# Strided items earlier in the middle heads, and the merge statistics and weights in the idle PSUM bank of a strided item

## The chip, the cores and the metric

One core of one Trainium2 chip runs the whole program. The metric is the device time of one execution in microseconds (us).

## The reference

The program computes one layer of a hybrid decoder for a prompt of 2048 tokens and for a small sample group. The stage that matters here is the prompt's attention: 8 heads of 64 channels, and in each head three branches of dilated window attention, which are merged by their softmax denominators.

```python
BRANCHES = ((128, 1), (512, 4), (2048, 16))
...
    s = jnp.einsum('bnqrhc,bnkrhc->bnrhqk', qb, kc).astype(jnp.float32)
    s = s * (HEAD_DIM ** -0.5) + bias[None, None, None]
    s = jnp.where(valid[None, :, None, None], s, NEG_INF)
    lse = jax.nn.logsumexp(s, axis=-1)
    p = jnp.exp(s - lse[..., None])
    o = jnp.einsum('bnrhqk,bnkrhc->bnqrhc', p.astype(vc.dtype), vc)
...
def _merge_branches(outs, lses):
    w = jax.nn.softmax(jnp.stack(lses, axis=0), axis=0)
    return jnp.sum(w[..., None] * jnp.stack(outs, axis=0).astype(jnp.float32), axis=0)
```

## The kernel before

The attention stage stands between the projections and the output projection with its feed-forward block. A head has 20 **items**: 16 *band* items, one for each block of 128 queries, which do the branches of dilation 1 and 4 together over up to five key blocks; and 4 *strided* items, which do the branch of dilation 16, each for four of its sixteen residues. The list `OTHER` (L1124) gives the order of the items of heads 1 to 6, `FIRST` and `LAST` those of heads 0 and 7. One item is begun at each step of a plan, so a head is 20 steps; "place 7" is below the eighth item of a head.

Every piece of work is filed with `at(step, phase, function)`, and the plan issues it sorted by step, then by phase (`early, exp, low, scores, turn, mid, values, out, misc, store`). Nothing else sets the order: each engine runs its instructions as they were issued, and waits in place for what is not ready.

An item begun at step x goes through these stages:

- **band**: scores on PE at x (L881); bias and minimum on DVE at x + 1 (L887); exponential on ACT at x + 2 (L892); transposes on PE at x + 3 (L900), in one group of up to four, and for every odd block from 4 on a second group of two; copies of the high parts on ACT (L903), and the low parts `pl` on DVE at x + 4 (L922). Every four band items their products with the values follow, in three parts on three steps (L936), then a copy to `ob` on ACT (L945).
- **strided**: queries put in order on POOL at x - 3 (L865, into one buffer `qo`); scores on PE at x (L954); bias and minimum on DVE at x + 1 (L959, L961) and the subtraction on POOL (L962); exponential on ACT at x + 3 (L965); sum on DVE (L969) and four transposes on PE (L974) at x + 4, with the high part `eh` on ACT (L977); the low part `el` on DVE at x + 5, phase `mid` (L922); the values on PE at x + 6 or the next step that no band values take (L985, L986); a copy to `o` on ACT one step later (L993).

PSUM: scores are written to `ps_s`, two buffers of two banks each in turn. A band item uses up to 640 columns of the pair; a strided item uses bank 0 alone, and its bank 1 is idle. All transposes go in turn to three single banks, named `ps_t0`, `ps_t1` and `ps_o2` (`ps_a`). The values have one bank, `ps_o3`.

When a head is done, its **statistics** (`Stats`: a product on POOL, two small matmuls on PE at L1012, a copy on DVE) and its **weights** (`Weights`: a minimum on DVE at L1030, small operations on POOL, ACT and DVE, a transpose on PE at L1051, a copy and a store to DRAM `f_d` on ACT) are made during the next head. They too take a bank of the three. The weights are then loaded again for all partitions (`merge_load`, SP's queue, L1067), and POOL multiplies and adds the two outputs in four chunks of three operations (`merge`, L1078, L1080, L1082); the result is stored to `cat_d` (L1087).

Of the kernel before, what the change touches and what calls it, by code (L numbers as in the profile page):

```python
# [21 lines left out]
NT = T // P  # L22
# [21 lines left out]
class Plan:  # L44
# [21 lines left out]
def hymba_step(ctx: ExitStack, tc: tile.TileContext, A: dict, O: dict):  # L66
    nc = tc.nc
    sync, act, dve, pool, pe = nc.sync, nc.scalar, nc.vector, nc.gpsimd, nc.tensor
# [7 lines left out]
    turn = [0, 0, 0, 0]  # L76
# [3 lines left out]
    def ps_s():  # L80
        return psum_s.tile([P, 2, 512], F32, name="ps_s", tag="s", bufs=2)
# [22 lines left out]
    def ps_a():  # L104

        turn[2] = (turn[2] + 1) % 3
        return bank(turn[2])
# [53 lines left out]
    at = plan.at  # L161
# [490 lines left out]
    B0 = 240  # L652
# [49 lines left out]
    for half in range(2):  # L702
        for ki, kind in enumerate(ORDER[half]):
            for gi, tiles in enumerate(GROUPS):
# [13 lines left out]
                for j, tj in enumerate(tiles):  # L718
                    t = half * 8 + tj
                    e, ph = e0 + 2 * j, "out"  # L720
                    if last:
                        e, ph = e0, "early"
                    elif third:

                        e, ph = (e0 + 2 * j + 2, "out") if j < 2 else (e0, "early")
# [41 lines left out]
    for i, (b, t, u) in enumerate(key_units):  # L767
        s0 = key_steps[i]
# [11 lines left out]
    for bg in range(2):  # L780
        s0 = V0 - 8 + bg * 33
# [164 lines left out]

    def strided_scores(it):
        d, st, r4 = it["d"], it["st"], it["n"]
        it["s"] = s = ps_s()[:, 0, :]
        for a in range(4):  # L950
            k = by_residue(d["k"])[:, r4 * 4 + a]
            out = s[:, a * P:(a + 1) * P].rearrange("p (n m) -> p n m", m=RUN)
            for z in range(2):
                pe.matmul(out, it["q"][:, z, a], k, start=(z == 0), stop=(z == 1))  # L954
# [45 lines left out]
    class Stats:  # L1000
# [5 lines left out]
            self.eng.tensor_tensor(self.m, self.st[:, 4:6].unsqueeze(3).broadcast_to([P, 2, NT, RUN]),  # L1006
                                   sel_m.unsqueeze(1).unsqueeze(1).broadcast_to([P, 2, NT, RUN]), op=OP.mult)

        def b(self):
            self.p = pt = ps_a()  # L1010
            for z in range(2):
                pe.matmul(pt[:, z * NT:(z + 1) * NT], self.m[:, z].rearrange("p r m -> p (r m)"), sel_n, start=True, stop=True)  # L1012

# [107 lines left out]


    FIRST = list(range(10)) + ["s", 10, 11, "s", 12, 13, "s", 14, 15, "s"]
    OTHER = [0, 1, "s", 2, 3, 4, 5, "s", 6, 7, 8, 9, "s", 10, 11, 12, 13, "s", 14, 15]  # L1124

    LAST = [0, "s", 1, "s", 2, "s", 3, "s", 4, 5, 6, 7] + list(range(8, NT))
    items, taken = [], set()
# [25 lines left out]
    for h in range(1, H):  # L1153
# [3 lines left out]
        for y in (6, 7, 8, 9, 11, 13) if h == 1 else (1, 2, 3, 4, 10, 12):  # L1157
            at(s0 + y, "misc", load, h)
        at(s0 + 16, "misc", order_bias, h)
    def stats_of(h, eng, steps):  # L1160
        d = {}
        at(*steps[0], lambda: d.update(s=Stats(h, sts[h], eng)))
        for (y, ph), fn in zip(steps, "abc"):
            at(y, ph, lambda fn=fn: getattr(d["s"], fn)())
        return d

    def weights_of(d, steps, n0=0, n1=NT):
        w = {}
        at(*steps[0], lambda: w.update(w=Weights(d["s"], n0, n1)))
        for (y, ph), fn in zip(steps, "weights_a weights_b weights_c weights_d weights_e turn store".split()):  # L1170
            at(y, ph, lambda fn=fn: getattr(w["w"], fn)())
        return w

    def steps_of(s0, *steps):
        return [(s0 + y, ph) for y, ph in steps]

    last_half = {}
    for h in range(H):

        s0 = B0 + (h + 1) * NI  # L1180
        end = h == H - 1
        ahead = h == H - 2
        if end:

            x = s0 - NI
            d = stats_of(h, dve, steps_of(x, (11, "misc"), (13, "early"), (14, "early")))
            weights_of(d, steps_of(x, (14, "misc"), (15, "early"), *[(15, "misc")] * 3, (16, "early"), (16, "exp")), 0, NT // 2)
            for ch in range(2):
                at(x + 17, "mid", merge_load, h, ch)
                for part in range(3):  # L1190
                    at(x + 19 + part, "store", merge, h, ch, pool, part)
            last_half = weights_of(d, steps_of(s0, (3, "early"), (4, "early"), *[(4, "misc")] * 3), NT // 2, NT)
            continue
        if ahead:
            d = stats_of(h, pool, steps_of(s0, (2, "misc"), (4, "early"), (5, "early")))
            weights_of(d, steps_of(s0, (5, "misc"), (6, "early"), (6, "misc"), (7, "early"), (7, "misc"), (8, "early"), (8, "mid")))
            chunks = ((10, 13), (10, 16))
        else:
            d = stats_of(h, pool, steps_of(s0, (3, "misc"), (5, "early"), (6, "early")))
            weights_of(d, steps_of(s0, (6, "misc"), (7, "early"), (7, "misc"), (8, "early"), (8, "misc"), (10, "early"), (10, "mid")))  # L1200
            chunks = ((13, 16), (13, 19), (19, 22), (22, 25))

        for ch, (a, b) in enumerate(chunks):
            at(s0 + a, "mid", merge_load, h, ch)
            for part in range(3):
                at(s0 + b + part, "store", merge, h, ch, pool, part)
        if ahead:
            at(s0 + 19, "store", merge_store, h, 0, 2)
        else:
            at(s0 + 28, "store", merge_store, h, 0, 4)  # L1210
    last_s = [0]
    for i, it in enumerate(items):
        x, h, n = B0 + i, it["h"], it["n"]
# [605 lines left out]
    h = H - 1  # L1819
# [333 lines left out]
```

## Time and profile before

| what | value |
|---|---|
| median of 3 runs | 2627.35 us (2621.5 to 2628.19) |
| profiled execution: its own time | 2623.9 us |
| profiled execution: span from first to last instruction | 2621.9 us |
| mean granted TensorE clock | 0.977 |
| PE, DVE, ACT, POOL busy, of the span | 95%, 54%, 47%, 53% |

The span is 2.0 us shorter than the time of the same execution; this rest lies around it. The attention stage is from about 600 to 920 us of the span, and one middle head takes about 39 us, with PE, DVE and ACT all above three quarters busy. In a row of the timeline the columns are start, duration, engine, line, operation, output and inputs, count; the bracket gives the engine's idle time before it and what ended that.

### The profile page before, as it was taken

What the parts mean: (1) busy time and instruction counts of PE and PEld (TensorE: products, weight loads), DVE (VectorE), ACT (ScalarE), POOL (GpSimd) and SP (SyncE); (2) the same over time, 40 slices, a digit from 0 to 9 for tenths busy, and PEclk for the clock granted to TensorE, in tenths of its full rate; (3) what the DMA queues carried; (4) which work ended last, traced back from release to release, by engine and by line L of the source; (5) the groups of instructions that cost most, each with busy time, mean ns of one, the idle gap of its engine ahead of it and who ended that gap; (6) DMA issues with size and microseconds to landing.
All of it is one profiled execution on the core that took longest, in us unless ns stands there. A gap on an engine that the chain in (4) does not pass through costs nothing. (4 is left out here: it accounts for less than half of the span.)

```text
span 2621.9 us, 38941 instructions
## 1 busy us (share of the span) xinstructions
PE 2480.9 (95%) x13583; PEld 2188.5 (83%) x13583; DVE 1414.6 (54%) x2770; ACT 1221.5 (47%) x2570; POOL 1382.9 (53%) x1080
## 2 busy tenths in 40 slices
PE   8999899999999869999999999999999999999996
PEld 6777687678888758898999988999999987999995
DVE  4258675346888846434444366444444466444445
ACT  6414344446877626545454545432323336434332
POOL 2035754123667646676776743554544534666662
PEclk9999899999999989999999999999999999999998
DMA  8764844588787565455464564554453643555553
GB/s 251 217 212 155 277 141 128 180 261 245 202 234 225 143 176 171 141 182 176 141 204 142 181 185 157 169 186 171 159 203 132 221 149 123 194 204 201 197 194 109
DMA packets 313874, 481.05 MB, mean 183 GB/s; under 512 B 25907, under 2 KB 178916, under 8 KB 307792
## 3 DMA queue, kind: packets, MB, share of 16 engines
q1 hardware_dynamic: 308188, 469.53, 56.4%
q10 hardware_dynamic: 5492, 9.05, 1.2%
q8 instruction: 108, 1.77, 0.3%
q14 instruction: 86, 0.70, 0.1%
HBM read 382.76 MB, written 165.84 MB: 209 GB/s over the span
## 5 line engine op out<-in xcount | busy, mean ns | idle before, releaser
L1585 POOL TENSOR_TENSOR op<-fr,op 128x512 fp32r<-128x512 f32 x385 | 488.4, 1300 | 299.9 <-ACT op L1581 275.3
L1642 PE MATMUL ps_m<-xh,op 128*128 128x384 f32 (+4 forms) x1932 | 615.5, 319 | 3.7 <-DVE zn L1663 3.7
L1644 PE MATMUL ps_m<-xh,op 128*128 128x384 f32 (+4 forms) x1932 | 615.1, 318 | 1.6 <-POOL op L1585 1.6
L1643 PE MATMUL ps_m<-xl,op 128*128 128x384 f32 (+4 forms) x1932 | 614.2, 318 | 0.0
L1715 PE MATMUL ps_o<-dw,hw 128*128 128x512 f32 x2040 | 487.1, 393 | 18.0 <-DVE acc L1717 16.7
L1715 PEld LDWEIGHTS ps_o<-dw,hw 128*128 128x128 f32 x2040 | 381.1, 189 | 102.1 <-DVE acc L1717 23.8
L1642 PEld LDWEIGHTS ps_m<-xh,op 128*128 128x128 f32 x1932 | 368.6, 191 | 8.3 <-issue 2.7
L1643 PEld LDWEIGHTS ps_m<-xl,op 128*128 128x128 f32 x1932 | 368.4, 191 | 3.6
L1644 PEld LDWEIGHTS ps_m<-xh,op 128*128 128x128 f32 x1932 | 368.2, 191 | 2.0 <-POOL op L1585 1.9
L1717 DVE TENSOR_TENSOR acc<-acc,ps_o 128x512 f32<-128x512 f32 (+1 forms) x362 | 247.1, 687 | 215.8 <-PE ps_o L1715 215.8
L1682 ACT ACTIVATE ps_t<-zn 128x384 f32<-128x384 f32 (+1 forms) x126 | 58.3, 463 | 470.4 <-DVE zn L1665 367.8
L1581 ACT ACTIVATE op<-fr 128x512 fp32r<-128x512 f32 x396 | 235.3, 623 | 22.5 <-DMA fr<-ab_d 15.1
L138 POOL TENSOR_TENSOR dw<-fd,dw 128x1024 fp32r<-128x1024 f32 x66 | 158.8, 2406 | 124.3 <-ACT dw L135 119.6
L318 PE MATMUL ps_s<-wh,xh 128*128 128x512 f32 x480 | 198.4, 413 | 6.3 <-ACT xh L135 6.1
L319 PE MATMUL ps_s<-wl,xh 128*128 128x512 f32 x480 | 192.3, 401 | 0.0
L320 PE MATMUL ps_s<-wh,xl 128*128 128x512 f32 x480 | 191.8, 400 | 0.0
L1585 POOL TENSOR_TENSOR op<-pair,op 128x512 fp32r<-128x512 f32 x63 | 81.4, 1300 | 120.4 <-ACT op L1581 120.4
L1692 ACT ACTIVATE hw<-ps_t 128x384 fp32r<-128x384 f32 (+1 forms) x126 | 56.0, 453 | 175.4 <-DVE ps_t L1688 174.4
L318 PEld LDWEIGHTS ps_s<-wh,xh 128*128 128x128 f32 x480 | 93.0, 194 | 36.2 <-issue 8.4
L320 PEld LDWEIGHTS ps_s<-wh,xl 128*128 128x128 f32 x480 | 92.9, 193 | 20.7 <-DVE xl L138 0.2
L319 PEld LDWEIGHTS ps_s<-wl,xh 128*128 128x128 f32 x480 | 93.5, 195 | 18.0 <-DVE wl L226 0.5
L611 POOL TENSOR_TENSOR vl<-kv,vh 100x512 fp32r<-100x512 f32 (+1 forms) x32 | 46.0, 1439 | 110.1 <-ACT vh L605 37.9
(473 smaller groups left out, 4794.2 us busy)
## 6 DMA issues: line engine op xcount, KB each, us to landing
fr<-ab_d SPq DMA_DIRECT2D x308, 256.0 KB
fd<-in_w_down_dram SPq DMA_DIRECT2D x66, 512.0 KB
out_ks_dram<-in_cache_k_dram SPq DMA_DIRECT2D x56, 512.0 KB
out_vs_dram<-in_cache_v_dram SPq DMA_DIRECT2D x56, 512.0 KB
ab_d<-fr SPq DMA_DIRECT2D x88, 256.0 KB
raw<-in_w_in_dram SPq DMA_DIRECT2D x72, 256.0 KB
qk_d<-pair SPq DMA_DIRECT2D x64, 256.0 KB
ab_d<-pair SPq DMA_DIRECT2D x63, 256.0 KB
```

Source lines behind the costliest of these rows:

```text
L138: (eng_lo or pool).tensor_sub(lo, src, hi.bitcast(F32))
L318: pe.matmul(o[j], xh[:, k, :], wh, start=(k == 0), stop=False)
L319: pe.matmul(o[j], xh[:, k, :], wl, start=False, stop=False)
L320: pe.matmul(o[j], xl[:, k, :], wh, start=False, stop=(k == KD - 1))
L1581: act.activation(ops[f, j][0], ab[f][j], AF.Copy)
L1585: (pool if f or j in POOL_LOW else dve).tensor_sub(lo_, ab[f][j], hi.bitcast(F32))
L1642: pe.matmul(out, wh[:, ks], xh[:, :, k], start=(k == 0), stop=False)
L1643: pe.matmul(out, wh[:, ks], xl[:, :, k], start=False, stop=False)
L1644: pe.matmul(out, wl[:, ks], xh[:, :, k], start=False, stop=(k == 3))
L1682: act.activation(g, c, AF.Silu)
L1715: pe.matmul(ps[0:nr], l_, r_[:, cs], start=(z == 0 and y == 0), stop=(z == FC - 1 and y == len(pairs) - 1))
L1717: dve.tensor_add(B.acc[i][0:nr, cs], B.acc[i][0:nr, cs], ps[0:nr])
```

## The change

It does three things.

1. `OTHER` is written in another order: the strided items of heads 1 to 6 stand at places 1, 6, 11 and 15 instead of 2, 7, 12 and 17.
2. The statistics' matmuls and the weights' transpose of heads 0 to 6 write bank 1 of the `ps_s` pair of a strided item of the running head, right behind that item's scores, instead of a bank of the three.
3. Statistics, weights, merges and their store move in the plan: for heads 1 to 5 the statistics begin at place 19 of their own head instead of place 3 of the next, the weights are stored at place 7 instead of 10, and the merges run three steps sooner; for head 0 the merges begin one step later.

```diff
     def strided_scores(it):
         d, st, r4 = it["d"], it["st"], it["n"]
-        it["s"] = s = ps_s()[:, 0, :]
+        it["pair"] = ps_s()
+        it["s"] = s = it["pair"][:, 0, :]
...
-        def b(self):
-            self.p = pt = ps_a()
+        def b(self, place=None):
+            self.p = pt = (place or ps_a)()
...
-    OTHER = [0, 1, "s", 2, 3, 4, 5, "s", 6, 7, 8, 9, "s", 10, 11, 12, 13, "s", 14, 15]
+    OTHER = [0, "s", 1, 2, 3, 4, "s", 5, 6, 7, 8, "s", 9, 10, 11, "s", 12, 13, 14, 15]
...
+    def strided_bank(y):
+
+        return lambda: items[y - B0]["pair"][:, 1, :]
+
-    def stats_of(h, eng, steps):
+    def stats_of(h, eng, steps, spare=False):
         d = {}
         at(*steps[0], lambda: d.update(s=Stats(h, sts[h], eng)))
         for (y, ph), fn in zip(steps, "abc"):
-            at(y, ph, lambda fn=fn: getattr(d["s"], fn)())
+            args = (strided_bank(y),) if spare and fn == "b" else ()
+            at(y, ph, lambda fn=fn, args=args: getattr(d["s"], fn)(*args))
         return d
...
-        if ahead:
-            d = stats_of(h, pool, steps_of(s0, (2, "misc"), (4, "early"), (5, "early")))
-            weights_of(d, steps_of(s0, (5, "misc"), (6, "early"), (6, "misc"), (7, "early"), (7, "misc"), (8, "early"), (8, "mid")))
-            chunks = ((10, 13), (10, 16))
+        if h == 0:
+            d = stats_of(h, pool, steps_of(s0, (3, "misc"), (6, "turn"), (7, "early")), True)
+            weights_of(d, steps_of(s0, (7, "misc"), (8, "early"), (8, "misc"), (9, "early"), (9, "misc"), (11, "turn"), (12, "early")), spare=True)
+            chunks = ((14, 17), (14, 20), (20, 22), (22, 25))
         else:
-            d = stats_of(h, pool, steps_of(s0, (3, "misc"), (5, "early"), (6, "early")))
-            weights_of(d, steps_of(s0, (6, "misc"), (7, "early"), (7, "misc"), (8, "early"), (8, "misc"), (10, "early"), (10, "mid")))
-            chunks = ((13, 16), (13, 19), (19, 22), (22, 25))
-
+            d = stats_of(h, pool, steps_of(s0, (-1, "misc"), (1, "turn"), (2, "early")), True)
+            weights_of(d, steps_of(s0, (2, "misc"), (3, "early"), (3, "misc"), (4, "early"), (4, "misc"),
+                                   (7 if ahead else 6, "turn"), (8 if ahead else 7, "early")), spare=True)
+            chunks = ((10, 13), (10, 16)) if ahead else ((10, 13), (10, 16), (16, 19), (19, 22))
...
-            at(s0 + 28, "store", merge_store, h, 0, 4)
+            at(s0 + (28 if h == 0 else 25), "store", merge_store, h, 0, 4)
```

In the rows that follow, the numbers behind a name tell buffers apart; a line number is that of the kernel the row is from, and in the changed kernel the lines behind L948 stand one higher.

**The statistics' matmuls on PE, early in a middle head.** Before, they follow the first part of the band values, and the scores of the next band item follow them:

```order
L936 MATMUL ps_o3_7079<-pl_6915,ve_6222 128x512
L1012 MATMUL ps_t1_7090<-sel_n_5422,sm_7065 128x16 x2
L881 MATMUL ps_s_7098<-k_6493,qh_6463 128x384
L881 MATMUL ps_s_7098<-k_6493,qh_6463 128x256
L881 MATMUL ps_s_7098<-k_6493,ql_6520 128x384
L881 MATMUL ps_s_7098<-k_6493,ql_6520 128x256
```

In the changed kernel:

```order
L936 MATMUL ps_o3_6956<-pl_6792,ve_6231 128x256
L955 MATMUL ps_s_6994<-k_6506,qo_6925 128x128 x8
L1013 MATMUL ps_s_6994<-sel_n_5422,sm_6961 128x16 x2
L900 MATMUL ps_t1_7005<-ident_76,e_6930 128x128 x4
```

They have moved four steps ahead, behind the scores of the strided item at place 1, and write the same `ps_s` pair.

**A strided item's transposes on PE, and who takes their bank next: place 7 before, place 6 now.** Before, the transposes write `ps_t0`, and the next to write `ps_t0` are the last two of these rows:

```order
L974 MATMUL ps_t0_7264<-ident_76,e3_7171 128x128 x4
L900 MATMUL ps_t1_7272<-ident_76,e_7204 128x128 x4
L936 MATMUL ps_o3_7222<-ph_7049,v_6765 128x256
L936 MATMUL ps_o3_7222<-pl_7050,v_6765 128x256
L936 MATMUL ps_o3_7222<-ph_7049,v_6765 128x128
L936 MATMUL ps_o3_7222<-pl_7050,v_6765 128x128
L954 MATMUL ps_s_7288<-k_6493,qo_7225 128x128 x8
L900 MATMUL ps_o2_7297<-ident_76,e_7232 128x128 x4
L900 MATMUL ps_t0_7303<-ident_76,e_7204 128x128
L900 MATMUL ps_t0_7303<-ident_76,e_7232 128x128
```

In the changed kernel the bank is `ps_o2`:

```order
L975 MATMUL ps_o2_6686<-ident_76,e3_6615 128x128 x4
L900 MATMUL ps_t0_6694<-ident_76,e_6643 128x128 x4
L900 MATMUL ps_t1_6700<-ident_76,e_6584 128x128
L900 MATMUL ps_t1_6700<-ident_76,e_6643 128x128
L936 MATMUL ps_o3_6674<-ph_6522,ve_6231 128x384
L936 MATMUL ps_o3_6674<-pl_6523,ve_6231 128x384
L955 MATMUL ps_s_6724<-k_5951,qo_6659 128x128 x8
L900 MATMUL ps_o2_6733<-ident_76,e_6666 128x128 x4
```

The odd band item, with its second group of two transposes, now falls into the strided item's own step, so its bank comes round one group sooner. On DVE the rows that lead to `el`, the operation that frees this bank, were

```order
L969 TENSOR_REDUCE st_6462<-e3_7171 128x4
L887 ISA e_7285,st_6462<-ps_s_7259,bp_6873 128x640
L887 ISA st_6462 128x1
L922 TENSOR_TENSOR pl_7182<-ps_t1_7272,ph_7181 128x4x128
L922 TENSOR_TENSOR el_7270<-ps_t0_7264,eh_7269 128x512
L959 TENSOR_TENSOR e3_7311<-ps_s_7288,b_6541 128x512
```

and are now, for the item at place 11 (the same rows stand at place 6, with L887 in the place of L960 and L962):

```order
L970 TENSOR_REDUCE st_5917<-e3_6747 128x4
L960 TENSOR_TENSOR e3_6855<-ps_s_6820,b_6000 128x512
L962 TENSOR_REDUCE st_5917<-e3_6855 128x4
L922 TENSOR_TENSOR pl_6792<-ps_t1_6837,ph_6791 128x4x128
L922 TENSOR_TENSOR pl_6792<-ps_o2_6843,ph_6791 128x256
L922 TENSOR_TENSOR el_6835<-ps_t0_6829,eh_6834 128x512
```

A second low part has come in ahead of `el` at places 6 and 11, and at place 11 also the next strided item's bias and minimum, which stood behind it.

**The last strided item's exponential on ACT: place 17 before, place 15 now.** Before, two transposed copies stand between the previous strided item's output copy (L993) and the exponential (L965):

```order
L993 ACTIVATE o3_7202<-ps_o3_7465 128x4x16x8
L903 ACTIVATE ph_7457<-ps_t0_7484 128x4x128
L903 ACTIVATE ph_7457<-ps_t1_7490 128x256
L965 ACTIVATE e3_7446<-e3_7446 128x512
L892 ACTIVATE e_7476,st_6462<-e_7476,st_6462 128x640
L892 ACTIVATE e_7507,st_6462<-e_7507,st_6462 128x640
L977 ACTIVATE eh_7533<-ps_o2_7528 128x512
```

In the changed kernel:

```order
L903 ACTIVATE ph_6791<-ps_t1_6893 128x4x128
L903 ACTIVATE ph_6791<-ps_o2_6899 128x256
L994 ACTIVATE o3_6641<-ps_o3_6903 128x4x16x8
L966 ACTIVATE e3_6855<-e3_6855 128x512
L892 ACTIVATE e_6885,st_5917<-e_6885,st_5917 128x640
L892 ACTIVATE e_6916,st_5917<-e_6916,st_5917 128x640
L978 ACTIVATE eh_6943<-ps_t0_6938 128x512
```

The output copy, which waits for the values on PE, has moved from ahead of the two copies to right ahead of the exponential.

More of the change, by code (lines that the diff above doesn't have):

```diff
@@ L1163, in stats_of, with weights_of @@
         for (y, ph), fn in zip(steps, "abc"):
-            at(y, ph, lambda fn=fn: getattr(d["s"], fn)())
+            args = (strided_bank(y),) if spare and fn == "b" else ()
+            at(y, ph, lambda fn=fn, args=args: getattr(d["s"], fn)(*args))
         return d
-    def weights_of(d, steps, n0=0, n1=NT):
+    def weights_of(d, steps, n0=0, n1=NT, spare=False):
         w = {}
@@ L1170, in weights_of @@
         for (y, ph), fn in zip(steps, "weights_a weights_b weights_c weights_d weights_e turn store".split()):
-            at(y, ph, lambda fn=fn: getattr(w["w"], fn)())
+            args = (strided_bank(y),) if spare and fn == "turn" else ()
+            at(y, ph, lambda fn=fn, args=args: getattr(w["w"], fn)(*args))
         return w
```

## The prediction

> **What bounds the kernel now.** I read the page's busy times first, then busy time by windows, then the waits, then the timeline of single places.
>
> ```profile
> PE 2480.9 (95%) x13583; PEld 2188.5 (83%) x13583; DVE 1414.6 (54%) x2770; ACT 1221.5 (47%) x2570; POOL 1382.9 (53%) x1080
> 731.11:770.13 39.02, 36.01 (x269) 33.16 (x268) 33.05 (x74) 30.77 (x73) 26.24 (x30) 1.00 0.82 227
> ```
>
> PE bounds the whole. The second row is one middle head (length; busy PE, PEld, DVE, ACT, POOL; clock; DMA share): PE is idle for 3.0 us of 39.0, DVE for 6.0, ACT for 8.3. So a middle head can lose at most 3 us of listed idle, and DVE and ACT are near enough to PE that the order inside a few us decides who waits. What PE waits for, in the five middle heads from 690 to 886 us (sum, times, longest):
>
> ```profile
> PE ps_t L900 <- DVE el L922: 3.8, 10, 0.5
> PE ps_t L1012 <- POOL sm L1006: 3.1, 4, 0.8
> PE ps_o L900 <- DVE el L922: 2.4, 5, 0.8
> PE ps_t L900 <- ACT e L892: 1.6, 5, 0.4
> PE ps_t L1051 <- DVE pl L922: 1.5, 3, 0.5
> PE ps_o L1051 <- DVE pl L922: 1.0, 2, 0.5
> PE ps_s L954 <- POOL qo L865: 1.0, 3, 0.6
> PE ps_o L900 <- ACT e L892: 0.8, 2, 0.4
> PE ps_o L1012 <- POOL sm L1006: 0.8, 1, 0.8
> ```
>
> Per head: 1.24 us for `el`, which frees a strided item's bank; 0.78 for the statistics' product `sm`; 0.50 for a bank at the weights' transpose; 0.48 for exponentials; 0.20 for queries. The sum is 16.0 us over five heads.
>
> **What is taken away.** In the changed order `sm` is done on POOL at step 19 and used by PE at step 21, in a bank that nobody holds, so the 0.78 and the 0.50 go. Is `sm` in time? Behind the last strided item's subtraction POOL has now the bias copy, two merge operations, two query copies, one merge operation and `sm`: 1.32 + 2 × 1.28 + 1.22 + 1.28 + 0.63 = 7.0 us, from about 1.5 us into step 16, and PE comes to it 5 steps of 1.95 (39.0 / 20) later: some 2 us spare. Were it late, the band transposes would stand behind it on PE, and on DVE the copy of the statistics and the strided bias. The 0.48 goes as well: one of its two places is ACT held up behind a store, the other is PE coming to transposes early:
>
> ```profile
> 737.85 0.60 ACT L945 ACTIVATE ob<-ps_o 128x512 f32<-128x512 f32 x1 [1.26 <-DMA cat_d<-ob]
> 739.31 0.66 PE L900 MATMUL ps_t<-ident,e 128*128 128x128 f32 x4 [0.25 <-ACT e L892]
> 768.34 0.65 PE L900 MATMUL ps_t<-ident,e 128*128 128x128 f32 x4 [0.43 <-ACT e L892]
> ```
>
> The store is now issued three steps (5.9 us) sooner, and behind the second place the strided values (0.92 us) now come first. On SP's queue two merge loads go ahead of the nine value loads instead of behind them; POOL waited for those loads, but nobody waits for POOL there, so this is worth nothing. Gain: 0.78 + 0.50 + 0.48 + 0.20 = 1.96 us a head, at most.
>
> **What is added: `el` comes later, its bank is wanted sooner.** The item at place 7, before:
>
> ```profile
> 732.72 0.63 ACT L965 ACTIVATE e<-e 128x512 f32<-128x512 f32 x1
> 733.24 0.83 ACT L892 ACTIVATE e<-e,st 128x640 f32<-128x640 f32 x1
> 734.69 0.83 ACT L892 ACTIVATE e<-e,st 128x640 f32<-128x640 f32 x1 [0.39 <-DVE pl L922]
> 734.76 0.60 PE L974 MATMUL ps_t<-ident,e 128*128 128x128 f32 x4
> 735.20 0.60 PE L900 MATMUL ps_t<-ident,e 128*128 128x128 f32 x4
> 735.52 0.58 ACT L977 ACTIVATE eh<-ps_t 128x512 fp32r<-128x512 f32 x1
> 735.55 0.37 PE L936 MATMUL ps_o<-ph,v 128*128 128x256 f32 x1
> 735.90 0.82 DVE L887 CUSTOM_DVE_ANT_0 e<-ps_s,bp 128x640 f32<-128x640 f32 x1
> 736.05 1.06 PE L954 MATMUL ps_s<-k,qo 128*128 128x128 f32 x8
> 736.64 0.69 DVE L922 TENSOR_TENSOR pl<-ps_t,ph 128x512 fp32r<-128x512 f32 x1
> 736.94 0.62 PE L900 MATMUL ps_o<-ident,e 128*128 128x128 f32 x4
> 737.24 0.68 DVE L922 TENSOR_TENSOR el<-ps_t,eh 128x512 fp32r<-128x512 f32 x1
> 737.84 0.68 DVE L959 TENSOR_TENSOR e<-ps_s,b 128x512 f32<-128x512 f32 x1
> 738.07 0.41 PE L900 MATMUL ps_t<-ident,e 128*128 128x128 f32 x2 [0.50 <-DVE el L922]
> 738.55 0.69 DVE L961 TENSOR_REDUCE st<-e 128x4 f32<-128x512 f32 x1
> 739.63 0.38 ACT L903 ACTIVATE ph<-ps_t 128x256 fp32r<-128x256 f32 x1
> 740.38 0.41 DVE L922 TENSOR_TENSOR pl<-ps_t,ph 128x256 fp32r<-128x256 f32 x1
> 741.85 0.50 PE L936 MATMUL ps_o<-ph,v 128*128 128x512 f32 x1
> 742.88 0.46 PE L881 MATMUL ps_s<-k,qh 128*128 128x384 f32 x2
> ```
>
> From start to start, PE has 2.6 us of work between L974 and the pair that wants the bank back (0.44, 0.35, 0.50, 0.89, 0.44), while `el` ends 3.16 us after L974: PE starts the pair 0.7 us late.
>
> *Place 6 now.* PE's work in between is 0.44 + 0.35 + 0.15 for the pair + 0.35 of values + 0.89 = 2.2 us: 0.4 less. DVE has one more low part (740.38 to 740.71: 0.33) and ACT one more copy (0.38) ahead of `el`. So 0.7 to 0.8 later. Further ahead PE stood 0.5 us at L1051 before, in which ACT drew level; without it the two exponentials of 0.8 us reach into the transposes: up to 0.5 more. I take +1.0.
>
> *Place 11 now.* L959 and L961 (0.71 + 0.60) stand ahead of `el` in the place of L887 (0.74), and the low part of 0.33: 0.9 later; PE has about as much work as before. DVE has some tenths to spare there: +0.6, between 0 and 0.9.
>
> *Place 15 now.* No strided scores stand between any more (0.89 less), but a full first part of values (741.85 to 742.88: 1.03) in the place of 0.72, and 0.18 for the scores of band 0: PE wants the bank 0.4 sooner. And the exponential now waits on ACT for the output copy of values that end on PE two score groups (1.3 us) ahead of the transposes; copy, exponential and one band exponential take 0.5 + 0.5 + 0.97: 0.3 to 0.6 late. I take +1.0, between 0.3 and 1.5.
>
> *Places 2 to 4.* The copy of the statistics, the minimum and the reciprocal of the weights, with the strided bias, now lie on DVE ahead of the low parts that the last band group's values need: +0.4, between 0 and 0.7. The minimum's price swings:
>
> ```profile
> L1030 DVE TENSOR_TENSOR f<-st x9: 159/882/3635, 649.7 to 930.7; 128x16 f32<-128x16 f32 x7, 128x8 f32<-128x8 f32 x2
> ```
>
> At 3.6 us it ran beside three POOL operations in a row. Now POOL's next operation behind the strided subtraction waits for this minimum itself, so I keep the middle one, 0.9. The Trainium skill's page "SBUF — State Buffer" (section "SBUF: two separate sides") says why: a DVE operation with two SBUF inputs and a GpSimd one exclude each other for whole instructions. The trace's 0.16 to 3.6 us agree; it would price a bad meeting at 2.7 us more.
>
> Behind each waiting group on PE stand values and the next scores, for which ACT and DVE wait in turn: a wait of PE here moves everything. Sum for a middle head: 1.0 + 0.6 + 1.0 + 0.4 - 1.96 = **+1.0 us**; for heads 1 to 6, +6 us. From the bounds: -1.96 + 0.3 (all at their low ends, place 6 at nothing) = -1.7 to -1.96 + 1.3 + 0.9 + 1.5 + 0.7 = +2.4 a head, so -10 to +15.
>
> **The edges.** Head 0's last strided items (steps 16, 19) now have the next at 21 instead of 22; its two waits go: 0. Where head 7 begins, its dense strided items met head 6's statistics:
>
> ```profile
> 879.68 0.62 PE L1012 MATMUL ps_t<-sel_n,sm 128*128 128x16 f32 x4 [0.85 <-POOL sm L1006]
> 881.87 3.63 DVE L1030 TENSOR_TENSOR f<-st 128x16 f32<-128x16 f32 x1
> 891.20 0.28 PE L1051 MATMUL ps_t<-ident,w 128*32 128x128 f32 x1 [1.57 <-POOL w L1047]
> ```
>
> Both waits go (2.4 us), and the minimum moves off; I add 1.1 for what DVE owed after it: -3.5, between -1 and -5.
>
> **The clock.**
>
> ```profile
> 630.00:650.00 20.00, 17.68 (x124) 16.41 (x124) 13.95 (x34) 11.91 (x28) 8.42 (x12) 0.91 0.98 276
> 633.55 0.32 PE L954 MATMUL ps_s<-k,qo 128*128 128x128 f32 x1 [0.95 <-POOL qo L865]
> 636.51 1.07 PE L974 MATMUL ps_t<-ident,e 128*128 128x128 f32 x4
> ```
>
> A granted clock of 0.91 over 20 us is 3.6 us at half rate; the same L974 takes 1.07 instead of 0.60. It came behind this wait of 0.95 and two more of 0.41 and 0.23 within 3 us. Such a stretch costs 1.8 us of PE. The new waits at places 6 and 15 are of that size, in twelve places: I take two more, **+4**, between 0 and 12. The page "TensorE: Matmul & The Clock Gate" (Trainium skill, "What's actually happening") says that the rate falls after an idle window of about 3.4 us. The stretch's length agrees; PE was never idle that long here.
>
> **Sum:** 6 - 3.5 + 4 = +6.5 us: the profiled execution's 2623.9 becomes 2630.4, and the median, which lies 3.4 us above it, 2633.9: **2634**.
>
> **The rivals.**
>
> 1. *The waits of `el` don't grow* (ACT and DVE draw level, since their work per head is the same and both have idle time): six times -1.96, less 3.5 at head 7: -15, cut to -10 by the tenths that already now go to `el`: **2617**. For it: 6 us of DVE idle a head. Against it: DVE and ACT are idle where PE stands, and two of the waits removed are such places.
> 2. *The half-rate clock decides*, slower: waits of 1.5 us and more in one place of each middle head, at places 6 or 15, let the clock fall in all six heads: 6 × 1.8 = 11 in the place of 4, and +3 for DVE then owing more, so 6 - 3.5 + 11 + 3 = +16: **2643**. It decides once PE idles about 1.5 us within 3 us.
> 3. *No clock stretch is added*, as the page's rule would have it: PE never stands still for 3.4 us in a middle head, the longest wait there is 0.8 now and some 1.7 then. Then 6 - 3.5 = +2.5: **2630**, no difference that can be told.
>
> **How the numbers follow.** What this kernel can be told apart by is about 0.3%, 7.9 us (2619.5 to 2635.2). The forecast has 0.42, its own range 2628 to 2640, half of it above 2635; rival 1 has 0.25, nearly all faster; rival 2 0.18, slower; rival 3 0.15, nearly all within. Faster 0.24, same 0.35, slower 0.41. The range from 2615 to 2645 takes in both outer cases' centres and leaves some 0.15 out.
>
> **What would show it.** Right, if the waits at lines 1013 and 1052 are gone in middle heads, if L900 waits for `el` for 3 us or more a head instead of 1.24, and if a middle head takes 39.5 to 40.5 us. The exponential of the last strided item should follow its neighbour's output copy directly. Wrong, if a head takes 38.5 or less, if `sm` or the weights still hold PE, or if the strided scores wait for POOL.

## The result, and the profile after

| | us | executions |
|---|---|---|
| before, median (range) | 2620.51 (2617.29 to 2632.16) | 20 |
| changed, median (range) | 2631.81 (2621.76 to 2646.13) | 20 |
| ratio, 95% interval | 1.0042 (1.0028 to 1.0055) | |

The change made the kernel slower by about 11 us. The profiled execution of the changed kernel is the quickest of its twenty (2621.76 us, granted clock 0.980), so its total is not typical. What it shows is read by stages, and heads are compared where the clock stood at 1.00 in both. The page's busy times, and one middle head from weights' transpose to weights' transpose (length; busy PE, PEld, DVE, ACT, POOL; clock; DMA share; GB/s):

```profile
PE 2478.8 (95%) x13583; PEld 2185.2 (83%) x13583; DVE 1417.4 (54%) x2770; ACT 1220.2 (47%) x2570; POOL 1383.4 (53%) x1080
731.86:771.91 40.05, 36.18 (x270) 33.18 (x269) 33.39 (x74) 30.70 (x72) 26.40 (x30) 1.00 0.84 221
```

The work is the same as before. The head is 40.05 us long where it was 39.02, and PE is idle for 3.87 of them where it was for 3.01. What PE waits for in the five middle heads from 690 to 886 us (sum, times, longest):

```profile
PE ps_t L900 <- DVE el L922: 9.5, 9, 1.5
PE ps_o L900 <- DVE el L922: 6.4, 6, 1.5
PE ps_s L881 <- DVE st L887: 2.1, 4, 0.5
PE ps_o L936 <- ACT o L994: 0.7, 1, 0.7
PE ps_t L900 <- ACT e L892: 0.5, 3, 0.2
```

The waits at the statistics' matmuls (3.9 us) and at the weights' transpose (2.5 us) are gone. The waits for `el` have grown from 6.2 to 15.9 us, that is from 1.24 to 3.2 us a head, and a wait of the scores for a bank that DVE is still reading in a band item's bias (`st`) is new. The four waits of one head, from the timeline of PE:

```profile
768.77 0.56 PE L881 MATMUL ps_s<-k,qh 128*128 128x384 f32 x2 [0.53 <-DVE st L887]
781.95 0.63 PE L900 MATMUL ps_t<-ident,e 128*128 128x128 f32 x4 [1.46 <-DVE el L922]
791.96 0.63 PE L900 MATMUL ps_t<-ident,e 128*128 128x128 f32 x4 [0.76 <-DVE el L922]
800.57 0.41 PE L900 MATMUL ps_t<-ident,e 128*128 128x128 f32 x2 [0.97 <-DVE el L922]
```

The three for `el` belong to the strided items of places 6, 11 and 15. Before, the item of place 7 cost 0.50 (the row at 738.07 us in the prediction), and those of places 12 and 17:

```profile
748.20 0.41 PE L900 MATMUL ps_t<-ident,e 128*128 128x128 f32 x2 [0.16 <-DVE el L922]
757.38 0.41 PE L900 MATMUL ps_o<-ident,e 128*128 128x128 f32 x2 [0.41 <-DVE el L922]
```

How the bank of place 6 comes to be late is seen on DVE, just ahead of the wait that ends at 781.95:

```profile
780.18 0.69 DVE L922 TENSOR_TENSOR pl<-ps_t,ph 128x512 fp32r<-128x512 f32 x1
780.79 0.41 DVE L922 TENSOR_TENSOR pl<-ps_o,ph 128x256 fp32r<-128x256 f32 x1
781.12 0.68 DVE L922 TENSOR_TENSOR el<-ps_t,eh 128x512 fp32r<-128x512 f32 x1
```

Two low parts of band items, for products that come later, stand ahead of the one operation for which PE is waiting.

The other heads went otherwise than the middle ones. Here a head is counted from its first scores on PE (the 128 columns of band item 0, L881), and the last stage ends with the first product behind the attention (L1642 before, L1649 now). The second profile is that of the run "changed kernel again" below; the forecast is without its term for the clock.

| stage | forecast | before, us | changed | changed, second profile |
|---|---|---|---|---|
| heads 1 and 2 | +2.0 | 77.0 | 86.5 | 89.0 |
| heads 3 to 6 | +4.0 | 156.5 | 161.8 | 160.2 |
| head 7 to the first product behind the attention | -3.5 | 162.5 | 155.0 | 155.5 |

The rows of the first and the last stage, first of the kernel before, then of the changed one (busy times as above):

```profile
636.09:713.10 77.01, 73.23 (x552) 69.07 (x553) 66.38 (x149) 63.14 (x148) 39.91 (x50) 0.98 0.72 213
869.58:1032.07 162.49, 127.89 (x653) 105.16 (x651) 97.14 (x187) 79.76 (x168) 98.92 (x88) 0.89 0.57 166
```

```profile
632.25:718.75 86.50, 76.45 (x550) 70.63 (x550) 68.31 (x149) 63.16 (x148) 47.55 (x58) 0.96 0.70 199
880.52:1035.56 155.04, 126.00 (x654) 103.64 (x653) 94.67 (x187) 79.62 (x169) 90.19 (x79) 0.91 0.56 168
```

So heads 1 and 2 lose most, and head 7 gains.

### The profile page after: what moved, and what is told of

Its sections match the earlier page's. It is cut to its first block, busy times and chain, and to the rows that moved or that the text cites. A ratio compares the mean times of both kernels' runs of the same rounds, so it can differ in the third digit from the quotient of the medians.

```text
span 2619.7 us, 38909 instructions
## 1 busy us (share of the span) xinstructions
PE 2478.8 (95%) x13583; PEld 2185.2 (83%) x13583; DVE 1417.4 (54%) x2770; ACT 1220.2 (47%) x2570; POOL 1383.4 (53%) x1080
## 5 line engine op out<-in xcount | busy, mean ns | idle before, releaser
L1649 PE MATMUL ps_m<-xh,op 128*128 128x384 f32 (+4 forms) x1932 | 614.9, 318 | 3.7 <-DVE zn L1670 3.7
L1649 PEld LDWEIGHTS ps_m<-xh,op 128*128 128x128 f32 x1932 | 368.3, 191 | 8.2 <-issue 2.7
```

Source lines behind the costliest of these rows:

```text
L1649: pe.matmul(out, wh[:, ks], xh[:, :, k], start=(k == 0), stop=False)
```

## The experiments

All runs of an experiment stand beside runs of the kernel before on the same chip: 12 executions each, but 6 of "order only" and 8 of the changed kernel. The table gives the median, the ratio with its 95% interval, and the mean difference to the kernel before of two quantities: *full rate*, the span times the granted clock, and *clock loss*, the span times one minus the clock (± one standard error). The split is rough, since a stretch at half rate in which PE waits anyway counts as loss and costs nothing.

| run | median us | ratio (95%) | full rate | clock loss | a middle head, us |
|---|---|---|---|---|---|
| changed kernel again | 2633.85 | 1.0044 (1.0026 to 1.0062) | +4.2 ± 1.1 | +6.4 ± 2.8 | 40.05 |
| order only | 2642.09 | 1.0072 (1.0054 to 1.009) | +13.5 ± 1.2 | +2.9 ± 1.9 | 41.14 |
| bank only | 2625.78 | 1.0017 (1.0004 to 1.0031) | -3.2 ± 1.1 | +6.5 ± 1.7 | 37.9 |
| changed, early low part | 2619.59 | 0.9977 (0.996 to 0.9994) | -10.3 ± 1.1 | +5.0 ± 2.5 | 36.8 |
| the same again | 2614.59 | 0.9971 (0.9955 to 0.9987) | -9.0 ± 1.3 | +1.0 ± 1.8 | 36.8 |
| before, early low part | 2621.34 | 0.9981 (0.9965 to 0.9998) | -4.9 ± 1.2 | +1.7 ± 1.8 | 38.55 |
| bank, early low part | 2621.65 | 0.9987 (0.9971 to 1.0002) | -7.5 ± 1.1 | +4.8 ± 2.0 | 38.0 |
| head 6 alone | 2629.28 | 1.0013 (0.9996 to 1.003) | +5.1 ± 1.3 | -1.4 ± 2.1 | 39.38 |
| changed, filled waits | 2629.02 | 1.0013 (0.9999 to 1.0027) | +10.6 ± 1.3 | -6.9 ± 1.8 | 40.05 |
| early low part, filled end | 2619.25 | 0.9976 (0.9962 to 0.999) | -2.0 ± 1.4 | -3.3 ± 2.2 | 36.8 |

The runs were made in three groups, each with the kernel before: the first four rows (its median 2623.01 us), then "before, early low part" to "changed, filled waits" (2623.78 us), then the repeated early low part and the filled end (2622.64 us).

**The changed kernel again**, as the neighbour of the first three.

> The changed kernel itself, beside the others on one chip: 40.0 us a middle head and 8 to 14 us above the kernel before, by both theories. For the clock: if the half-rate stretches are a part of the price, its mean granted clock lies below that of the kernel before in the same rounds by 0.001 to 0.003, which is 3 to 8 us; if they are not, the clocks are equal and all of the price stands in the heads' lengths.

The difference of 10.8 us is there again, with 4.2 us of it at full rate and 6.4 us in the clock.

**Order alone.** The kernel before with the new order; the weights' transpose is one step sooner, so that it stays clear of the strided items.

```diff
-    OTHER = [0, 1, "s", 2, 3, 4, 5, "s", 6, 7, 8, 9, "s", 10, 11, 12, 13, "s", 14, 15]
+    OTHER = [0, "s", 1, 2, 3, 4, "s", 5, 6, 7, 8, "s", 9, 10, 11, "s", 12, 13, 14, 15]
...
-            weights_of(d, steps_of(s0, (6, "misc"), (7, "early"), (7, "misc"), (8, "early"), (8, "misc"), (10, "early"), (10, "mid")))
+            weights_of(d, steps_of(s0, (6, "misc"), (7, "early"), (7, "misc"), (8, "early"), (8, "misc"), (9, "early"), (9, "mid")))
```

> The kernel before with the new order of OTHER alone (strided items at places 1, 6, 11, 15); statistics, weights and merges stay as they were, in one of the three banks, with the weights' transpose one step sooner. Theory (the order makes a strided item's low part late): a middle head takes 40.0 us or more in place of 39.0, PE waits 3 us or more a head for it, the waits for the statistics' product stay (0.8 a head); the time is 8 to 16 us above the kernel before. Rival (the earlier statistics and merges do the harm): a middle head stays at 39.0, the time within 3 us of the kernel before.

It is the slowest of all: a middle head takes 41.14 us, 2.1 more than before, and the median is 19 us higher, beyond the 8 to 16 that were expected. The waits of PE from 690 to 886 us:

```profile
PE ps_t L900 <- DVE el L922: 13.6, 10, 2.1
PE ps_o L900 <- DVE el L922: 4.6, 4, 2.1
PE ps_t L1051 <- POOL w L1047: 3.7, 3, 1.2
PE ps_o L1051 <- POOL w L1047: 2.5, 2, 1.2
```

The waits for `el` are 18.2 us, three times those before, with the statistics and the weights still in the three banks. The waits for `sm`, which were expected to stay, are not among them any more. So it is the order that makes `el` late, and not the use of the idle bank. The row L1051 belongs to the earlier step of the weights in this experiment, 1.24 us a head, and is no part of the change.

**Bank alone.** The old order, with statistics and weights turned in the idle bank; both had to be filed some two steps sooner, and the merges of heads 1 to 5 start two steps sooner.

```diff
-            d = stats_of(h, pool, steps_of(s0, (3, "misc"), (5, "early"), (6, "early")))
+            d = stats_of(h, pool, steps_of(s0, (1, "misc"), (3 if ahead else 2, "turn"), (4 if ahead else 3, "early")), True)
...
-            chunks = ((13, 16), (13, 19), (19, 22), (22, 25))
+            chunks = ((10, 13), (10, 16)) if ahead else ((11, 14), (11, 17), (17, 20), (20, 23))
```

> The old order (places 2, 7, 12, 17) with the statistics and weights in the idle bank of a strided item's scores and in earlier steps, as in the change. Theory: the two waits of 1.3 us a head go and the low part is wanted when it always was; a middle head takes 37.9 to 38.7 us, the time is 2 to 7 us below the kernel before. Rival (those two waits were the ones in which DVE and ACT drew level, so they come back as waits for the low part): 39.0 a head, the time equal within 2 us.

A middle head takes 37.9 us, 1.1 less than before, close to the 1.28 us by which the prediction priced the two waits that go. Yet the whole is not faster, where 2 to 7 us less were expected. Heads 1 to 3, from first scores to first scores, take 125.6 us where they took 116.5, with 13.7 us at half rate where it was 3.4; heads 4 to 6 gain 3.2 us. In head 2 a wait of 2.7 us comes up, behind a copy on ACT that waits for a merge on POOL, and in head 3 one of 1.7 us for `sm`. The clock's record falls right behind each, for 3.4 us:

```profile
700.70 0.60 ACT L994 ACTIVATE o<-ps_o 128x512 f32<-128x512 f32 x1 [2.75 <-POOL ob L1083]
701.35 0.50 PE L936 MATMUL ps_o<-ph,ve 128*128 128x512 f32 x1 [2.66 <-ACT o L994]
728.49 0.62 PE L1013 MATMUL ps_s<-sel_n,sm 128*128 128x16 f32 x4 [1.74 <-POOL sm L1007]
```

In a middle head order and bank seem to add up: +2.1 and -1.1 are +1.0, and the changed kernel has +1.03. That is luck in part, since the +2.1 hold the 1.24 us at L1051, which the changed kernel does not have.

**The low part first.** If the waits for `el` are the loss, it should be enough to let DVE make `el` at the start of its step, ahead of the band items' low parts and the next bias. One word is changed in the changed kernel:

```diff
-            at(x + 5, "mid", low_parts, it)
+            at(x + 5, "low", low_parts, it)
```

> The changed kernel with a strided item's low part ahead of the band items' low parts of its step on DVE, instead of behind them; nothing else. Theory (the bank's reader stands behind one or two band low parts): it comes 0.6 to 0.9 us sooner at places 6, 11 and 15, a middle head falls from 40.0 to 38.5 to 39.3 us, the time 5 to 9 us below the changed kernel. Rival (ACT's copy of the high part is what is late): a middle head stays at 39.7 or more, since the low part waits for ACT wherever it stands.

> The changed kernel with the low part of a strided item at the start of its step, once more, as the neighbour of the next run on the same chip. If its gain is real: median 2617 to 2622 us, ratio 0.996 to 0.9995, PE's waits for el between 690 and 886 us under 2 us (15.9 in the changed kernel), one middle head 36.9 us. If the first measurement was luck of the clock: ratio 0.999 to 1.002.

It beats both kernels, in two measurements of 12 executions each: 2619.59 and 2614.59 us, 0.2 to 0.3% below the kernel before and 0.5% below the changed one in the same group (2619.59 against 2633.85). The gain is larger than expected: 14 us for 5 to 9, and a middle head of 36.8 us for 38.5 to 39.3. A middle head and its waits, and the place of the 1.46 us again:

```profile
729.85:766.66 36.81, 35.83 (x270) 33.19 (x270) 32.84 (x73) 30.59 (x72) 26.43 (x30) 1.00 0.94 241
```

```profile
PE ps_s L881 <- DVE st L887: 2.0, 4, 0.5
PE ps_o L936 <- ACT o L994: 1.9, 3, 0.7
PE ps_t L900 <- DVE el L922: 0.9, 3, 0.3
```

```profile
774.72 0.69 DVE L922 TENSOR_TENSOR el<-ps_t,eh 128x512 fp32r<-128x512 f32 x1
775.32 0.68 DVE L922 TENSOR_TENSOR pl<-ps_t,ph 128x512 fp32r<-128x512 f32 x1
775.55 0.63 PE L900 MATMUL ps_t<-ident,e 128*128 128x128 f32 x4 [0.31 <-DVE el L922]
775.92 0.41 DVE L922 TENSOR_TENSOR pl<-ps_o,ph 128x256 fp32r<-128x256 f32 x1
```

`el` now goes ahead of the two low parts; the wait is 0.31 in the place of 1.46 us, and nobody waits for the low parts that come later. PE is idle for 0.98 us of the head, and the head is 3.2 us shorter than in the changed kernel.

**The same word in the kernel before, and with the bank alone.**

> The kernel before with one phase changed: the low part of a strided item's exponentials is made on VectorE at the start of its step instead of its middle. Nothing else of the change is in it. Theory (the low part is late in either order, and only the step phase of it decides): the 6.2 us of waits of L900 for el between 690 and 886 us fall to under 2 us, while the waits at the merge transposes (L1012 about 0.8, L1051 about 0.5 us a head) stay; span times clock falls by 4 to 6 us against the kernel before, to about 2554 us, ratio 0.997 to 0.999. Rival (the gain of the early low part needs the order and the idle bank of the changed kernel, since there it was late by 1 us a place and here only by 0.3 to 0.8): no change, ratio 0.999 to 1.002.

> The old order of the middle heads, the statistics and weights turned in the idle bank, and the low part of a strided item at the start of its step. Theory (bank and order are separate terms, and the low part's phase a third): the 5.2 us of waits for el of the kernel with the bank alone fall to under 2 us; its 6.9 us of waits of L936 for the output copy stay; span times clock about 2551 to 2553 us, ratio 0.996 to 0.999, close to the changed kernel with the early low part (2549 us). Rival (the place of the strided items decides once the low part is early): its median is 5 us or more above the 2619.6 us of that kernel.

Both keep the old order. In the kernel before the waits for `el` are gone from 690 to 886 us, but at most 0.5 us of the 1.24 a head is kept (heads 3 to 6 together take 156.6 us for 156.5, with one stretch of 3.4 us at half rate that was not there before); PE now comes sooner to `sm` and to the exponentials (0.78 and 0.25 before):

```profile
738.80 0.66 PE L900 MATMUL ps_t<-ident,e 128*128 128x128 f32 x4 [0.58 <-ACT e L892]
761.10 0.62 PE L1012 MATMUL ps_o<-sel_n,sm 128*128 128x16 f32 x4 [1.51 <-POOL sm L1006]
```

With the bank alone it is worth nothing in a head (38.0 for 37.9 us), for the same reason:

```profile
PE ps_o L936 <- ACT o L994: 6.3, 4, 3.4
PE ps_s L1013 <- POOL sm L1007: 5.4, 4, 1.8
```

At full rate both came where they were expected. But the early low part is worth 3.2 us a head with the new order and half a microsecond or less with the old one, where it gives the time to the next wait. The medians of all kernels with an early low part lie within 7 us, and only the middle heads (36.8 us against 38.0 and 38.55) tell them apart clearly.

**Head 6 alone.** The new order, bank and plan for head 6 only, to measure what the prediction put down for the start of head 7.

> The kernel before, with the changed order, idle bank and plan for head 6 alone; the heads up to 5 are those of before. It isolates the term of the prediction for the start of head 7 (-3.5 us, -1 to -5). Theory: the stage up to the last merge is 3 to 4.6 us shorter, span times clock about 2555 to 2557 us against 2559.5 us, ratio 0.998 to 1.0. Rival (the gain at head 7 was a half-rate stretch that the kernel before happened to have there): no change in span times clock, ratio 0.999 to 1.001.

The expected gain did not come: the median is 5.5 us higher, and the full rate 5.1 ± 1.3 us higher. In the profile, the 5.7 us by which the span is longer all lie ahead of the first strided scores (at 619.96 us against 614.25), where the two kernels do the same; from there to the first product behind the attention it takes 417.7 us against 417.8. Inside this stage the term looked for is there: from the first scores of head 7 on it takes 157.0 us where it took 162.5, 5.5 less. But head 6, the first in the new order, takes 42.4 us where it took 38.8, and heads 1 and 2, planned as before, 80.0 for 77.0, with 3.4 us more at half rate. Why the full rate of the whole program is higher is not shown. The first strided scores start at different times in executions of one program as well (610.9 and 614.7 us in two profiles of the changed kernel).

**The clock.** Two runs ask what calls the half rate. In the first, eight transposes of the identity are put in at steps 11 and 16 of heads 1 to 6 of the changed kernel, that is into the waits for `el` of the items at places 6 and 11 (1.46 and 0.76 us). In head 1 they overwrite the transposed weights of head 0 before ACT copies them, so the merge of head 0 works with other numbers at the same cost.

```diff
+    def filler(it):
+        for a in range(8):
+            pe.transpose(it["pair"][:, 1, a % 4 * P:(a % 4 + 1) * P], ident, ident)
...
+    for h in range(1, H - 1):
+        at(B0 + h * NI + 11, "turn", lambda h=h: filler(items[h * NI + 11]))
+        at(B0 + h * NI + 16, "turn", lambda h=h: filler(items[h * NI + 15]))
```

> The changed kernel plus eight transposes of the identity into the idle bank, ahead of the transposes of el that wait behind places 11 and 15 of heads 1 to 6: 96 added TensorE operations of about 0.07 us, 0.5 us a place, inside waits of 1.0 to 1.5 us. Their output is used by nothing. Theory of the clock term (TensorE waiting about 1.5 us in 3 us calls the half-rate stretches): the loss, span times one minus clock, falls from 66 us by 4 us or more, to the 62 us of before, at the same span times clock or up to 1 us more. Rival (the stretches come whatever TensorE waits there): the loss stays within 2 us of that of the changed kernel, and the time is the same or up to 4 us longer.

The clock loss is 13.3 us below that of the changed kernel (-6.9 against +6.4, each to its own group's kernel before), and the ratio is 1.0013 in the place of 1.0044, though PE does 1.65 us more of work in each head (37.83 busy in 40.05 us; that is 0.8 us a place and not the 0.5 expected). That is the direction of the theory. Of the 13.3 us, 6.4 come back at full rate, where at most 1 was expected. It can't be pinned to the filled places: in the profile of this run the clock stands at 1.00 from 646 to 926 us, but so it does in the second profile of the changed kernel, unfilled, from 652 to 924.

```profile
652.00:924.00 272.00, 241.98 (x1780) 220.75 (x1779) 224.74 (x488) 206.21 (x484) 173.47 (x198) 1.00 0.72 194
```

The second run goes to a place where every profile shows a half-rate stretch: the end of the attention, where PE waits for the last merge. This is the kernel with the early low part (timeline of PE, and the window behind the wait):

```profile
937.46 0.39 PE L1401 MATMUL ps_m<-op,accm 128*128 128x512 f32 x1
944.73 0.79 PE L1399 MATMUL ps_m<-op,xh 128*128 128x512 f32 x1 [6.88 <-ACT xh L1390]
945.33 0.63 PE L1400 MATMUL ps_m<-op,xh 128*128 128x512 f32 x1
```

```profile
942.00:955.00 13.00, 7.33 (x16) 5.05 (x17) 6.32 (x5) 1.46 (x3) 7.56 (x6) 0.51 0.37 98
```

```diff
-        for i in (1, 2, 0):
+        for i in (1, 2):
             open_part(B, i, (KD - 1,), False, True)
+        idle = open_bank(B, 3)
+        for a in range(56):
+            pe.transpose(idle[:, a % 4 * P:(a % 4 + 1) * P], ident, ident)
+        open_part(B, 0, (KD - 1,), False, True)
+        for a in range(24):
+            pe.transpose(idle[:, a % 4 * P:(a % 4 + 1) * P], ident, ident)
```

> The same, plus 56 and 24 transposes of the identity into an unused bank while TensorE waits for the last merge at the end of the attention (6.9 and 2.9 us idle in the profile of the kernel without them, after which its products take 0.43 us each in the place of 0.23 from 944.7 to 955.6 us, at a recorded clock of 0.5 from 941.6 to 955.2). Their output is overwritten by the products that follow. Theory (idleness of TensorE calls the half rate): the record there stays at 1.0, the products behind the wait take 0.23 us from the first on, the loss, span times one minus clock, falls by 3 to 7 us, and the median by 3 to 6 us, to about 2614 to 2617 us. Rival (the half rate comes at this place whatever TensorE does, or for the change of load when work begins again): the record falls there all the same, the loss stays within 2 us, and the median is within 2 us of the kernel beside it.

```profile
945.81 6.28 PE L1922 MATMUL ps_m<-ident 128*128 128x128 f32 x56
951.84 0.48 PE L1399 MATMUL ps_m<-op,xh 128*128 128x512 f32 x1
952.16 0.40 PE L1400 MATMUL ps_m<-op,xh 128*128 128x512 f32 x1
967.88 0.79 PE L1399 MATMUL ps_m<-op,xh 128*128 128x512 f32 x1 [6.61 <-ACT xh L1390]
```

```profile
946.00:961.00 15.00, 14.85 (x107) 13.41 (x105) 5.36 (x5) 1.46 (x3) 7.32 (x6) 1.00 0.46 104
964.00:974.00 10.00, 4.83 (x11) 3.35 (x12) 5.72 (x7) 3.07 (x6) 6.95 (x7) 0.55 1.08 315
```

With PE kept busy, the record stays at 1.00 and the same products take 0.40 us in the place of 0.63. So at this place it is the idle time that calls the half rate. The clock loss is 4.3 us lower (-3.3 against +1.0), which is not clear of noise, as the standard error of the difference is 2.8. And the median is not lower (2619.25 against 2614.59, with intervals of the ratios that overlap): PE comes sooner to its next wait, which is now 6.6 us long and unfilled, and there the clock falls all the same. In the kernel without the filling, the product at 944.73 waits for an operand that ACT copies (L1390) from one that DVE makes, and DVE itself had stood for 8.33 us until a load had landed:

```profile
943.00 1.33 DVE L1387 TENSOR_TENSOR raw<-xl,xh 128x128 f32<-128x128 f32 x1 [8.33 <-DMA raw<-f_d]
```

So this stretch ends when the loads end, and PE's rate matters little in it.

## Why the prediction was right, point by point

Forecast and sign were right: 2634 us, where two medians were 2631.81 and 2633.85. That the number came so close is luck in part. The difference was put too small, +6.5 us, and came out as +11.3 and +10.8; the three executions known beforehand had a median of 2627.35, some 4 to 7 us above those of the later, larger groups, and this made up for it. And two terms were off by several microseconds in opposite directions: heads 1 and 2, and head 7.

- **What is taken away** held. The 0.78 and 0.50 us are gone in the middle heads, and the exponentials' 0.48 is down to 0.1 (0.5 us in five heads). `sm` was ready in time. The experiment with the bank alone confirms the size, 1.1 us in a middle head.
- **`el` at places 6 and 11** held to a tenth: +1.0 and +0.6 predicted, 1.46 - 0.50 = +0.96 and 0.76 - 0.16 = +0.60 measured, by the mechanism named: low parts ahead of it on DVE.
- **`el` at place 15** was mis-sized: +1.0 predicted, 0.97 - 0.41 = +0.56 measured (within the bounds of 0.3 to 1.5). The exponential does follow its neighbour's output copy, as said:

```profile
755.35 0.60 ACT L994 ACTIVATE o<-ps_o 128x512 f32<-128x512 f32 x1 [0.19 <-PE ps_o L987]
755.85 0.62 ACT L966 ACTIVATE e<-e 128x512 f32<-128x512 f32 x1
```

- **Places 2 to 4** had the right size, at another line. +0.4 was expected as a wait of the values for low parts; it came as 0.53 us at the scores, which wait for DVE to read the bank, behind the weights' reciprocal.

```profile
768.04 0.25 DVE L1044 RECIPROCAL f<-f 128x16 f32<-128x16 f32 x1 [0.85 <-POOL f L1041]
768.21 0.49 DVE L887 CUSTOM_DVE_ANT_0 e<-ps_s,bp 128x384 f32<-128x384 f32 x1
```

- **The sum of a middle head**, +1.0 us, was measured as 40.05 - 39.02 = +1.03, or +0.9 against the mean of heads 3 to 6 before, which are 38.8 to 39.5 us long. Both sides came out a little smaller: the four terms give 0.96 + 0.60 + 0.56 + 0.53 = 2.65 where 3.0 was put, and the gains are 1.86 for 1.96 by the listed waits. That makes +0.8, and PE's own busy time grew by 0.17 (36.18 for 36.01).
- **Heads 1 and 2** are the step that failed. "For heads 1 to 6, +6 us" gives them the sum of a middle head, +2.0 for both, and the end of head 0 is put at 0; they came out at +9.5 and +12.0. What the change takes away is hardly there in them: before, from 636 to 713 us, PE waits once for 0.50 us at the weights' transpose, never for `sm`, and 0.3 us for exponentials. What it adds is there in full: 5.6 us of waits for `el` in the place of 2.6, 1.5 us once in head 1 (L1103, transposes for the small sample group), and in head 2 the wait of places 2 to 4 with 1.76 in the place of 0.53 us:

```profile
686.04 0.57 PE L881 MATMUL ps_s<-k,qh 128*128 128x384 f32 x2 [1.76 <-DVE st L887]
```

There DVE stands 2.09 us ahead of the weights' reciprocal, for small operations on POOL between which two merge operations stand (L1083 and L1079, 1.29 us each); by the plan these are head 0's, whose merges begin one step later while the weights of head 1 are made sooner. In all, PE is idle for 10.05 us of the two heads (9.42 in the second profile) where it was for 3.78, and its own work takes 3.2 and 6.4 us longer, with more of it at half rate.
- **The start of head 7** was mis-sized: -3.5 us was put, between -1 and -5, and the stage from there came out at -7.4 and -7.0. The two waits named (0.85 and 1.57 us) did go, and the minimum took 0.17 us in the place of 3.63. A wait of 2.64 us of strided values for an output copy on ACT, which the forecast does not name, fell to 0.2, and the clock's record stood at one half for 27.3 us in the place of 34.1. Against this, the strided scores now wait for DVE and POOL (0.73 and 0.55 us), and the last values 2.59 us for their low part, where it was 0.5.
- **The clock**, +4 us, was of the right order, +6.4 ± 2.8 by the mean clocks, but not at the place named, so the size is luck too. In heads 1 to 6, with the stretch at the start of head 1 counted whole, the record stands at one half for 3.4 us before, and for 10.2 and 17.1 us in the two profiles of the changed kernel. Only one stretch of 3.4 us lies in a middle head, behind the 1.46 us wait (822 to 827 us), and that head is 41.67 us long in the place of 40.05; the other middle heads have the same wait and no stretch, and neither has any middle head in the second profile. The rest lies at the start of heads 1 and 2: 3.4 us at 632.0, 3.4 us behind the wait of 1.76 us, and 17.1 us in the second profile, in which PE is busy for 16.2:

```profile
635.40:652.50 17.10, 16.21 (x74) 15.43 (x75) 8.56 (x19) 8.91 (x20) 5.81 (x8) 0.50 0.79 273
```

And the clock loss rises as much with the bank alone, +6.5 ± 1.7, where the waits for `el` are as short as before (5.2 us for 6.2) and other waits have come up. So the waits for `el` are not shown to be the trigger, a wait of 1.46 us is not enough by itself, and what calls the stretches stays open. The page "TensorE: Matmul & The Clock Gate" of the Trainium skill ("What's actually happening") asks for an idle window of about 3.4 us. The filled end of the attention agrees with it, since the record falls some 4 us after PE goes idle there and not at all when PE is kept busy. The stretch at 822 us does not, for nothing there was idle for longer than 1.5 us.
- **The rivals.** That `el` would not grow later (2617) fell with 15.9 us of waits. That the half-rate clock decides (2643) asked for a stretch at places 6 or 15 of every middle head; the profiles show one in the first and none in the second. It is nearer in single executions, whose clock went down to 0.970. That no stretch is added (2630) fits the total of the first profile, in which heads 1 to 6 have more of the half rate and head 7 and what follows as much less, and not that of the second (44.4 us at half rate from head 1 on, where both others have 37.5).
- **Against "DVE has 6 us of idle time a head".** The prediction set this aside, and the early low part shows why: no work had to be saved on DVE. The same operations in another sequence are worth 3.2 us a head.

## What to carry to other kernels

When a bank is wanted sooner, look at what stands ahead of the operation that frees it on its own engine, and file that operation first; here it was worth 3.2 us a head, and taking the bank's other users away 1.1. A wait that is removed is kept only if the next engine in line has spare time: the same edit gained 3.2 us a head in one order and half a microsecond in another. And an order that is slower by itself can be the better one to build on. A price worked out for a middle head holds for middle heads: the first heads and the last want rows of their own.

## What the runs showed that was not expected

- Idle time can cost twice: behind a wait of 6.88 us the products took 0.63 us in the place of 0.40 for some 11 us (944.7 to 955.6 us, the clock's record at 0.51). Transposes with no use, put into the wait, kept the rate up. They did not pay here, where the next wait was not PE's own. But idle time is not all: in the second profile of the changed kernel the record stood at 0.50 for 17.1 us with PE busy for 16.2 of them.
- Executions of one kernel differ by some 19 us in the clock's loss alone (the changed kernel in the first group: 2641.0 us at 0.971 and 2625.7 us at 0.978, so 76.6 and 57.8 us lost), and by 3.8 us in when the attention starts. Changes of a few microseconds have to be read from a stage at a clock of 1.00, not from medians.
- The minimum of the weights (128x16, two SBUF inputs on DVE) took 0.16 to 1.24 us in the changed kernel, where it had reached 3.6 us before:

```profile
L1031 DVE TENSOR_TENSOR f<-st x9: 156/727/1235, 649.3 to 934.9; 128x16 f32<-128x16 f32 x7, 128x8 f32<-128x8 f32 x2
```
